# Attention with q left unnormalised: its reciprocal root as a per-row scale of the scores

## The chip, the cores and the metric

The kernel runs on one core of one Trainium2 chip. The metric is the device time of one execution in microseconds. Engines are named as in the profile: PE (TensorE matmul), PEld (its weight loads), DVE (VectorE), ACT (ScalarE), POOL (GpSimd) and SP (SyncE, which issues the transfers here).

## What is computed

The reference is a model of four layers on 1040 tokens (16 meta tokens and 1024 others), width 1024: attention, a matrix LSTM, a gated linear recurrence, attention again. The change touches the two attention layers. In them, cut to what matters:

```python
def rmsnorm(x, g):
    y = x * lax.rsqrt(jnp.mean(x * x, axis=-1, keepdims=True) + EPS)
    return y * g

q, k, v, z = split(u @ w_in)              # 16 q heads, 4 k/v heads of 64
q = rope(rmsnorm(q, q_gain), pos)
k = rope(rmsnorm(k, k_gain), pos)
s = einsum(q, kk) * 64 ** -0.5            # window of 128, blocks of 128 queries
s = where(mask, s, -inf)
m = maximum(s.max(-1), sink)
e = exp(s - m)
p = e / (e.sum(-1) + exp(sink - m))
o = einsum(p, vv)
out = (o * silu(z)) @ w_out
```

The normalisation is per head and per token: over the 64 values of one head.

## The kernel before

Activations lie with features on partitions and tokens along the row. Tokens are cut into three chunks of 400, 384 and 256 columns (`CHUNKS`; the last layer computes q from column 16 on, so its chunks are 384, 384 and 256), and into nine blocks: 16 meta tokens and eight of 128 (`CHUNK_BLOCKS` has four, three and two of them in the three chunks). Every large product is made of three fp32r products of a high and a low part, `proj` at L227: 24 instructions for a tile of 128 features and one chunk.

A q tile (there are eight per attention layer) holds two heads of 64 features. Its way through `qk_proj`, per chunk:

- `evac`: ACT copies the product times the gain column into `dst` (L491) and squares it into `sq` (L492); SP then issues four copies of 32 partitions each into `rot` (L495), the other half of each head for the rope. `dst`, `sq` and `rot` are three of the six buffers of the pool "t" (`tmp`, `TMPS`), which other stages use too.
- `stat`: one f32 product (L506) of a block matrix of ones, 128 x 128, with the squares sums each head's 64 squares and spreads the sum over the head's 64 partitions; ACT makes the reciprocal root in two activations over the whole chunk (L337 Ln, L338 Exp). The first `stat` of a chunk also loads the rope factors `cs` (L503), which have one buffer.
- `rope`: four passes of DVE: times cosine (L511), rotated times sine (L512), sum (L513), times the reciprocal root (L514).
- `q_split`: the high part (ACT, L462) and the low part (DVE, L463), for the two heads, into "qs" buffers (four per chunk size).

K tiles, two per layer, take the same way with their own split (L443 to L446).

The mixers then take, per pair of q tiles, block and head, an `S_step`: four products of q with k (L597, L598) into one PSUM tile, a copy of the sinks by POOL (L602), then for each of the two heads one pass of DVE (L604) that adds the mask, multiplies by -1.0 and takes the minimum with the negated sink, giving the negated scores and minus the maximum; ACT makes the exponential and its sum (L607), DVE the reciprocal (L609), POOL the product (L610). `T_step` transposes (L622) and splits the result (L624, L625); `V_step` multiplies with v (L641).

The order of PE's work is written out as a list of steps, each with a cost in ns (`MM` is 1/2.4 ns a column). Finishing steps are events: `D_Q` gives, in booked ns of PE work behind the end of a tile's projection, when `stat`, `rope` and the split stand. `spread`, `chain` and `weave` put events and fills between the steps; the loop at L723 moves a split behind the last `S_step` that still uses its buffers. Only PE runs in exactly this order (L115); the queues of the other engines are ordered at build time, by the order of the steps, with the mixers' steps raised (`hi`, `PRIO`), and by when their inputs and buffers are ready in the builder's model.

Of the kernel before, what the change touches and what calls it, by code (L numbers as in the profile page):

```python
# [9 lines left out]
F32 = mybir.dt.float32  # L10
F32R = mybir.dt.float32r
AF = mybir.ActivationFunctionType
ALU = mybir.AluOpType
PSUM = bass.MemoryType.PSUM

P = 128
# [7 lines left out]
BIG = -1.0e30  # L24
CHUNKS = [(0, 400), (400, 384), (784, 256)]
LAST_CHUNKS = [(16, 384), (400, 384), (784, 256)]
CHUNK_BLOCKS = [(0, 1, 2, 3), (4, 5, 6), (7, 8)]


def blk(b):  # L30
    return (0, NMETA) if b == 0 else (NMETA + P * (b - 1), P)
# [14 lines left out]
D_V, V_AHEAD, K_AHEAD = 1500.0, 3000.0, 12000.0  # L46
PARTS = 4
FIRST = (0.2, 0.8, 0.85), (0.2, 0.75, 0.8)
D_Q = 2000.0, 4000.0, 6000.0


MM = 1.0 / 2.4
# [58 lines left out]
def hybrid_kernel(ctx: ExitStack, tc: tile.TileContext, ins, out, layers=(0, 1, 2, 3)):  # L111
    nc = tc.nc
    v, s, g, pe, sp = nc.vector, nc.scalar, nc.gpsimd, nc.tensor, nc.sync
# [11 lines left out]
    def nm(x):  # L125
        ctr[0] += 1
        return f"{x}{ctr[0]}"
# [22 lines left out]
    def psa():  # L150
        return psum("pa", 1)
# [7 lines left out]
    eps = cpool.tile([P, 1], F32, name="eps")  # L159
# [19 lines left out]
    def new_mix():  # L179
        if layer_pool[0] is not None:  # L180
            layer_pool[0].close()
        layer_pool[0] = ExitStack()
        return layer_pool[0].enter_context(tc.tile_pool(name=nm("mix"), bufs=1))
# [231 lines left out]
    def layer_a(i, j, first, last, fin):  # L415
        win, wout = ins["a_win"][j], ins["a_wout"][j]
        chunks = LAST_CHUNKS if last else CHUNKS
        R = {}

        def enter():  # L420
            R["mix"] = mix = new_mix()
            R["masks"] = masks = mix.tile([P, 384], F32, name=nm("masks"))
            sp.dma_start(masks, ins["a_masks"])
            R["cons"] = cons = mix.tile([P, 18], F32, name=nm("cons"))
            sp.dma_start(cons, ins["a_cols"][j])
            v.tensor_scalar(cons[:, 0:1], cons[:, 0:1], 0.125, None, op0=ALU.mult)
            v.tensor_scalar(cons[:, 2:18], cons[:, 2:18], -1.0, None, op0=ALU.mult)

        order = {}
# [22 lines left out]
        def q_split(t):  # L452


            def step(qf, n, c0, cn):
                def fn():
                    q = qf()
                    R["q", t, n] = []
                    for hh in range(2):
                        st = R["mix"].tile([P, CHUNKS[n][1]], F32R, tag=f"qs{n}", name=nm("qs"), bufs=4)  # L460
                        hs, os = slice(64 * hh, 64 * hh + 64), slice(64 - 64 * hh, 128 - 64 * hh)
                        s.copy(st[hs, :cn], q[hs])  # L462
                        v.tensor_tensor(st[os, :cn], q[hs], st[hs, :cn].bitcast(F32), op=ALU.subtract)  # L463
                        R["q", t, n].append(st)

                order["q", t, n] = z = [0.0, fn, None]
                return z

            return step
# [12 lines left out]

            return work

        def qk_proj(src, gcol, work, fsplit, ch):
            late = {}

            def evac(acc, n, c0, cn):
                dst, sq, rot = work(n, c0, cn)
                late[n] = dst, sq, rot  # L490
                s.activation(dst, acc[:, :cn], AF.Identity, scale=R["cons"][:, gcol : gcol + 1])  # L491
                s.activation(sq, acc[:, :cn], AF.Square)  # L492
                for q in range(4):
                    o = q ^ 1
                    sp.dma_start(rot[32 * q : 32 * q + 32], dst[32 * o : 32 * o + 32])  # L495

            def finish(n, c0, cn):
                def stat():
                    dst, sq, rot = late[n]
                    b0, bn = CHUNKS[n]  # L500
                    if R.get("cs", (None,))[0] != n:
                        R["cs"] = n, R["mix"].tile([P, 2, 400], F32, tag="cs", name=nm("cs"), bufs=1)
                        sp.dma_start(R["cs"][1][:, :, :bn], ins["rope"][:, :, b0 : b0 + bn].rearrange("a p t -> p a t"))  # L503
                    late[n] = dst, sq, rot, R["cs"][1][:, :, c0 - b0 : c0 - b0 + cn]
                    st = psa()
                    pe.matmul(st[:, :cn], R["masks"][:, 0:P], sq, start=True, stop=True)  # L506
                    rstd_from(st, sq, cn, 64)

                def rope():
                    dst, sq, rot, cos_sin = late[n]  # L510
                    v.tensor_tensor(dst, dst, cos_sin[:, 0, :cn], op=ALU.mult)  # L511
                    v.tensor_tensor(rot, rot, cos_sin[:, 1, :cn], op=ALU.mult)  # L512
                    v.tensor_tensor(dst, dst, rot, op=ALU.add)  # L513
                    v.tensor_tensor(dst, dst, sq, op=ALU.mult)  # L514

                return [(D_Q[0], [4 * cn * MM, stat, None]), (D_Q[1], [0.0, rope, None]),
                        (D_Q[2], fsplit(lambda: late[n][0], n, c0, cn))]

            return proj(src, evac, ch), [finish(n, *c) for n, c in enumerate(ch)]

# [51 lines left out]
        def mixers():  # L572


            def S_step(w):
                mix, cons = R["mix"], R["cons"]
                b, hh, n = w["b"], w["hh"], w["n"]
                kh, kl = R["k", w["pair"] // 2][hh]
                q0, nq = blk(b)
                qb = slice(q0 - chunks[n][0], q0 - chunks[n][0] + nq)  # L580
                if b == 0:
                    k0, kbs = 0, ((0, 0, 16),)
                elif b == 1:
                    k0, kbs = 0, ((0, 0, 16), (1, 16, 128))
                else:
                    k0, kbs = q0 - P, ((b - 1, 0, 128), (b, 128, 128))
                w["kbs"] = kbs
                nk = sum(z[2] for z in kbs)
                kw, mo = (nk if b == 0 else 256), {0: 128, 1: 112}.get(b, 0)
                kb = slice(k0, k0 + kw)  # L590
                S = psum("pm", 2).rearrange("p (u k) -> p u k", u=2)
                w["Sm"] = Sm = mix.tile([P, 2, 257], F32, tag="Sm", name=nm("Sm"), bufs=2)
                st, den = small(2), small(2)
                sinks = []
                for u, t in enumerate(w["ts"]):
                    q = R["q", t, n][hh]
                    pe.matmul(S[:nq, u, :kw], q[:, qb], kh[:, kb], start=True, stop=False)  # L597
                    pe.matmul(S[:nq, u, :kw], q[:, qb], kl[:, kb], start=False, stop=True)  # L598
                    head = (2 * (t // 4) + hh) * 4 + t % 4
                    sinks.append(cons[:nq, 2 + head : 3 + head])  # L600
                    if u == 0:
                        g.tensor_copy(Sm[:nq, :, nk : nk + 1], cons[:nq, 2 + head : 4 + head].rearrange("p (u c) -> p u c", c=1))  # L602
                for u in range(2):
                    v.tensor_tensor_reduce(Sm[:nq, u, :nk], S[:nq, u, :nk], R["masks"][:nq, P + mo : P + mo + nk],  # L604
                                           -1.0, sinks[u], ALU.add, ALU.min, st[:nq, u : u + 1])
                for u in range(2):
                    s.activation(Sm[:nq, u, : nk + 1], Sm[:nq, u, : nk + 1], AF.Exp, scale=-1.0,  # L607
                                 bias=st[:nq, u : u + 1], accum_out=den[:nq, u : u + 1])
                v.reciprocal(den[:nq], den[:nq])  # L609
                g.tensor_tensor(Sm[:nq, :, :nk], Sm[:nq, :, :nk],  # L610
                                den[:nq].rearrange("p (u c) -> p u c", c=1).to_broadcast([nq, 2, nk]), op=ALU.mult)
# [41 lines left out]
            for pair in range(4):  # L653
                for b in range(1 if last else 0, NB):
                    n = [b in z for z in CHUNK_BLOCKS].index(True)
# [3 lines left out]
            for k in range(len(units) + V_LAG):  # L659
                seg = units[k]["pair"] if k < len(units) else 4  # L660
                for lag, cost, fn in ((V_LAG, 480, V_step), (T_LAG, 432, T_step), (0, 480, S_step)):
                    if 0 <= k - lag < len(units):
                        w = units[k - lag]
# [10 lines left out]
        kg1, kfin1 = qk_proj(win[1], 1, tmps, k_split(1), CHUNKS)  # L674
        vg0, vfin0 = v_proj(win[2], 0)
        vg1, vfin1 = v_proj(win[3], 1)
        qg = {t: qk_proj(win[4 + t], 0, tmps, q_split(t), chunks) for t in range(8)}

        def q_pair(p):

# [42 lines left out]
        for i in range(3, 12):  # L723
            for t in (2 * (i // 3), 2 * (i // 3) + 1):
                at = [id(z) for z in body]
                q, k = (at.index(id(z)) if id(z) in at else -1
                        for z in (order["q", t, i % 3], order["S", i // 3 - 1, i % 3]))
# [623 lines left out]
    ahead, k = 0.0, 0  # L1351
# [6 lines left out]
    k = 0  # L1358
# [31 lines left out]
def _layout(inp):  # L1390
    f = {}
# [3 lines left out]
    am = np.zeros((P, 384), np.float32)  # L1395
    am[:64, :64] = 1.0
    am[64:, 64:128] = 1.0
    ii = np.arange(P)[:, None]
    jj = np.arange(256)[None]
    am[:, 128:] = np.where((jj > ii) & (jj <= ii + P), 0.0, BIG)  # L1400
    f["a_masks"] = am
    f["b_mask"] = np.where(ii <= np.arange(P)[None], 0.0, BIG).astype(np.float32)
    f["ident"] = np.eye(P, dtype=np.float32)
# [7 lines left out]
    for j in range(2):  # L1411
        w = np.asarray(inp["a_w_in"])[j]
# [7 lines left out]
        qg, kg = np.asarray(inp["a_q_gain"])[j], np.asarray(inp["a_k_gain"])[j]  # L1420
# [7 lines left out]
    q0, k0, v0, i0, f0, o0, z0 = np.cumsum([0, 1024, 1024, 2048, 8, 8, 2048])  # L1428
# [27 lines left out]
    masks = np.zeros((P, 6, 32), np.float32)  # L1456
# [22 lines left out]
```

## Time and profile before

| | |
|---|---|
| three runs, us | 2633.74, 2634.56, 2635.0 |
| median | 2634.56 us |
| profiled execution, span from first to last instruction | 2630.8 us, 53986 instructions |
| mean granted clock of PE | 0.995 |
| layer 0 (attention) | about 0 to 445 us of the span |
| layer 3 (attention) | about 2200 us to the end |

For the profiled execution the profile gives the span; no other time of it is known. The span lies 3.8 us under the median of the runs.

How to read it: times are in us from the span's start, unless marked ns. A group line reads: line of the kernel, engine, operation, output <- inputs by the program's names, shape, count | busy us in all, mean ns of one | idle time of the engine just before them and what ended most of it. A line of the waits reads: who waited <- for whom: us in all, times, longest. In order of time: start, duration, engine, line, operation, and in brackets the engine's idle time before it and what ended it. Matmuls are pipelined: one lasts longer than the distance to the next.

### The profile page before, as it was taken

The page shows a single profiled execution, that of the slowest core. Times are in us where ns is not written, and L with a number is a line of the kernel's source. Part 1 is how long each engine was busy: PE and PEld are TensorE (multiplying, and loading weights), DVE is VectorE, ACT ScalarE, POOL GpSimd, SP SyncE. Part 2 cuts the span into 40 slices and gives each one's busy share as a digit, 9 for nine tenths or more (in the row PEclk, how much of TensorE's full clock was granted, in tenths as well). Part 3 has the DMA queues.
Part 4 walks back from the last instruction along what each step waited for, and adds up shares of the span by engine and source line. Part 5 has one row for each costly group of instructions (what it writes and reads, how often), then busy time and mean ns, then how long its engine had stood idle before and what let it go on. Part 6 is the DMA issues. An engine that isn't in the chain of part 4 may idle for free.

```text
span 2630.8 us, 53986 instructions
## 1 busy us (share of the span) xinstructions
PE 2562.9 (97%) x20246; PEld 2468.6 (94%) x20246; DVE 1976.8 (75%) x5344; ACT 1693.7 (64%) x4374; POOL 249.5 (9%) x502
## 2 busy tenths in 40 slices
PE   7999999989999999999999999999999999999999
PEld 5899989989999999999999999999999998999999
DVE  7887798784747474757475688988888989887896
ACT  7777767565454545454545757878675857867772
POOL 2221231000000000000000000101000000321330
PEclk9999999999999999999999999999999999999999
DMA  4213111011111111111111101111110113212112
GB/s 129 69 49 91 47 44 48 22 63 52 41 57 41 57 41 57 41 53 45 53 45 49 53 30 42 34 34 34 38 38 30 38 50 92 63 39 83 55 37 80
DMA packets 82581, 135.89 MB, mean 52 GB/s; under 512 B 12032, under 2 KB 35712, under 8 KB 82320
## 3 DMA queue, kind: packets, MB, share of 16 engines
q1 hardware_dynamic: 82320, 132.45, 15.9%
q8 instruction: 159, 2.61, 0.4%
q14 instruction: 102, 0.84, 0.1%
HBM read 117.56 MB, written 4.26 MB: 46 GB/s over the span
## 4 chain that ended last, share of the span: by engine, by line
PE 74%; DVE 12%; ACT 8%; DMA 3%; issue 2%; SPq 1%; POOL 1%; DVEq 0%; ACTq 0%; POOLq 0%
PE pj L227 35%; PE pj L321 15%; PE pj L276 10%; ACT Sm L607 1%; PE po L641 1%; PE po L885 1%; PE pt L622 1%; PE pa L899 1%; PE po L887 1%; DVE Sm L604 1%; DVE wl L194 1%; DMA cs<-in_rope 1%; PE pj L272 1%; DVE Pl L625 1%; PE pm L1137 1%
## 5 line engine op out<-in xcount | busy, mean ns | idle before, releaser
L227 PE MATMUL pj<-uh,wh 128*128 128x256 f32 (+2 forms) x2688 | 919.7, 342 | 9.4 <-ACT uh L193 9.4
L227 PE MATMUL pj<-ul,wh 128*128 128x256 f32 (+2 forms) x2688 | 867.2, 323 | 2.7 <-DVE ul L194 2.4
L227 PE MATMUL pj<-uh,wl 128*128 128x256 f32 (+2 forms) x2688 | 863.8, 321 | 0.0
L227 PEld LDWEIGHTS pj<-uh,wh 128*128 128x128 f32 x2688 | 509.3, 189 | 28.6 <-ACT uh L193 13.1
L227 PEld LDWEIGHTS pj<-ul,wh 128*128 128x128 f32 x2688 | 509.5, 190 | 13.8 <-DVE ul L194 6.4
L227 PEld LDWEIGHTS pj<-uh,wl 128*128 128x128 f32 x2688 | 509.0, 189 | 0.1
L193 ACT CAST wh<-wr 128x512 fp32r<-128x512 f32 (+1 forms) x338 | 202.9, 613 | 102.0 <-PE pj L321 31.3
L194 DVE TENSOR_TENSOR wl<-wr,wh 128x512 fp32r<-128x512 f32 (+1 forms) x338 | 232.1, 697 | 48.5 <-ACT wh L193 45.0
L321 PE MATMUL pj<-yh,wh 128*128 128x384 f32 (+2 forms) x768 | 253.1, 330 | 9.9 <-DVE x L324 6.4
L324 DVE TENSOR_TENSOR x<-x,pj 128x384 f32<-128x384 f32 (+2 forms) x480 | 234.6, 509 | 34.1 <-PE pj L321 32.7
L321 PE MATMUL pj<-yl,wh 128*128 128x384 f32 (+2 forms) x768 | 245.3, 319 | 0.3 <-DVE yl L194 0.3
L321 PE MATMUL pj<-yh,wl 128*128 128x384 f32 (+2 forms) x768 | 245.2, 319 | 0.0
L276 PE MATMUL pj<-wh,uh 128*128 128x256 f32 (+1 forms) x768 | 231.9, 302 | 0.0
L276 PE MATMUL pj<-wl,uh 128*128 128x256 f32 (+1 forms) x768 | 216.5, 282 | 0.0
L276 PE MATMUL pj<-wh,ul 128*128 128x256 f32 (+1 forms) x768 | 216.2, 281 | 0.0
L607 ACT ACTIVATE Sm<-Sm,s 128x257 f32<-128x257 f32 (+2 forms) x272 | 130.7, 482 | 91.7 <-DVE s L604 90.3
L610 POOL TENSOR_TENSOR Sm<-Sm,s 128x512 f32<-128x512 f32 (+2 forms) x136 | 141.2, 1038 | 467.1 <-DVE s L609 454.3
L403 ACT ACTIVATE t<-t 128x384 f32<-128x384 f32 (+2 forms) x240 | 117.8, 491 | 88.0 <-DVE t L402 86.4
L402 DVE SCALAR_TENSOR_TENSOR t<-pj,t 128x384 f32<-128x384 f32 (+2 forms) x192 | 98.8, 515 | 81.7 <-ACT t L401 80.0
L321 PEld LDWEIGHTS pj<-yh,wh 128*128 128x128 f32 x768 | 144.2, 188 | 14.7 <-DVE x L324 8.6
L193 ACT CAST yh<-r 128x384 fp32r<-128x384 f32 (+2 forms) x120 | 57.1, 478 | 146.2 <-PE pj L321 132.5
L276 PEld LDWEIGHTS pj<-wh,uh 128*128 128x128 f32 x768 | 144.6, 188 | 2.1
(251 smaller groups left out, 5445.7 us busy)
## 6 DMA issues: line engine op xcount, KB each, us to landing
wr<-in_b_win SPq DMA_DIRECT2D x124, 256.0 KB, 2.8
wr<-in_a_win SPq DMA_DIRECT2D x80, 256.0 KB, 2.9
wr<-in_c_win SPq DMA_DIRECT2D x64, 256.0 KB, 2.8
wr<-in_a_wout SPq DMA_DIRECT2D x32, 256.0 KB, 2.8
wr<-in_b_wout SPq DMA_DIRECT2D x32, 256.0 KB, 2.7
t<-t SPq DMA_DIRECT2D x104, 48.0 KB, 2.0
cs<-in_rope SPq DMA_DIRECT2D x11, 400.0 KB, 3.7
cs<-in_rope SPq DMA_DIRECT2D x11, 384.0 KB, 3.2
```

Of the source, the lines that this page charges most:

```text
L193: s.copy(h, src)
L194: v.tensor_tensor(l, src, h.bitcast(F32), op=ALU.subtract)
L227: pe.matmul(acc[:, :cn], a[:, k, :], b[:, k, c0 : c0 + cn], start=(k == 0 and i == 0), stop=(k == KT - 1 and i == 2))
L272: pe.matmul(acc[:48, :nc], um[0][:, k, :], m[:, kk, :], start=(k == 0 and m is wh), stop=(k == KT - 1 and m is wl))
L276: pe.matmul(acc[:cn, :nc], a[:, k, c0 : c0 + cn], m[:, kk, :], start=(k == 0 and j == 0), stop=(k == KT - 1 and j == 2))
L321: pe.matmul(acc[:, :cn], a[:, k, mc], b, start=(k == 0 and i == 0), stop=(k == 1 and i == 2))
L324: v.tensor_tensor(x[:, m, c0 : c0 + cn], x[:, m, c0 : c0 + cn], acc[:, :cn], op=ALU.add)
L402: v.scalar_tensor_tensor(a[:, :cn], z, 0.0, a[:, :cn], op0=ALU.min, op1=ALU.subtract)
L403: s.activation(a[:, :cn], a[:, :cn], AF.Exp)
L604: v.tensor_tensor_reduce(Sm[:nq, u, :nk], S[:nq, u, :nk], R["masks"][:nq, P + mo : P + mo + nk], -1.0, sinks[u], ALU.add, ALU.min, st[:nq, ...
L607: s.activation(Sm[:nq, u, : nk + 1], Sm[:nq, u, : nk + 1], AF.Exp, scale=-1.0, bias=st[:nq, u : u + 1], accum_out=den[:nq, u : u + 1])
L610: g.tensor_tensor(Sm[:nq, :, :nk], Sm[:nq, :, :nk], den[:nq].rearrange("p (u c) -> p u c", c=1).to_broadcast([nq, 2, nk]), op=ALU.mult)
```

## The change

Per q tile and chunk the reciprocal root is no longer multiplied into q. `rope` and the split work on the unnormalised q, and the score pass multiplies each query's row by that query's reciprocal root. For that the sums of squares have to lie with queries on partitions: `stat_q` takes, for each block of 128 tokens, the squares of that block as the stationary operand and two columns of the block matrix (one per head) as the moving one, so that one column per head and block comes out; the two activations run on these columns, two per block, into `rq`. The sign that the score pass gave by -1.0 moves into the gain column (-0.125), and the mask's constant is positive. The loading of the rope factors becomes a step of its own, `factors`, and q has four event times of its own; K keeps the three old ones.

```diff
-D_Q = 2000.0, 4000.0, 6000.0
+D_K = 2000.0, 4000.0, 6000.0
+D_Q = 1500.0, 2500.0, 3500.0, 4500.0
...
-            v.tensor_scalar(cons[:, 0:1], cons[:, 0:1], 0.125, None, op0=ALU.mult)
+            v.tensor_scalar(cons[:, 0:1], cons[:, 0:1], -0.125, None, op0=ALU.mult)
...
+                def stat_q():
+
+                    sq = late[n][1]
+                    nb = len(CHUNK_BLOCKS[n])
+                    R["rq", t, n] = rq = R["mix"].tile([P, 2 * nb], F32, tag=f"rq{n}", name=nm("rq"), bufs=4)
+                    st = psa()
+                    for k, b in enumerate(CHUNK_BLOCKS[n]):
+                        if last and b == 0:
+                            continue
+                        q0 = blk(b)[0] - c0
+                        pe.matmul(st[:, 2 * k : 2 * k + 2], sq[:, q0 : q0 + P], R["masks"][:, 0:P:64], start=True, stop=True)
+                    z = slice(2 if last and n == 0 else 0, 2 * nb)
+                    s.activation(rq[:, z], st[:, z], AF.Ln, bias=eps, scale=1.0 / 64)
+                    s.activation(rq[:, z], rq[:, z], AF.Exp, scale=-0.5)
...
-                    v.tensor_tensor(dst, dst, sq, op=ALU.mult)
-
-                return [(D_Q[0], [4 * cn * MM, stat, None]), (D_Q[1], [0.0, rope, None]),
-                        (D_Q[2], fsplit(lambda: late[n][0], n, c0, cn))]
+                    if t is None:
+                        v.tensor_tensor(dst, dst, sq, op=ALU.mult)
+
+                turn = fsplit(lambda: late[n][0], n, c0, cn)
+                if t is not None:
+                    return [(D_Q[0], [0.0, factors, None]), (D_Q[1], [108 * len(CHUNK_BLOCKS[n]), stat_q, None]),
+                            (D_Q[2], [0.0, rope, None]), (D_Q[3], turn)]
+                return [(D_K[0], [4 * cn * MM, stat, None]), (D_K[1], [0.0, rope, None]), (D_K[2], turn)]
...
                 for u in range(2):
+                    rq = R["rq", w["ts"][u], n][:nq, 2 * kq + hh : 2 * kq + hh + 1]
                     v.tensor_tensor_reduce(Sm[:nq, u, :nk], S[:nq, u, :nk], R["masks"][:nq, P + mo : P + mo + nk],
-                                           -1.0, sinks[u], ALU.add, ALU.min, st[:nq, u : u + 1])
+                                           rq, sinks[u], ALU.add, ALU.min, st[:nq, u : u + 1])
...
-    am[:, 128:] = np.where((jj > ii) & (jj <= ii + P), 0.0, BIG)
+    am[:, 128:] = np.where((jj > ii) & (jj <= ii + P), 0.0, -BIG)
```

More of the change, by code (lines that the diff above doesn't have):

```diff
@@ L483, in work_rows, with qk_proj @@
             return work
-        def qk_proj(src, gcol, work, fsplit, ch):
+        def qk_proj(src, gcol, work, fsplit, ch, t=None):
             late = {}
@@ L497, in finish, with factors @@
             def finish(n, c0, cn):
-                def stat():
-                    dst, sq, rot = late[n]
+                def factors():
                     b0, bn = CHUNKS[n]
@@ L503, in stat @@
                         sp.dma_start(R["cs"][1][:, :, :bn], ins["rope"][:, :, b0 : b0 + bn].rearrange("a p t -> p a t"))
-                    late[n] = dst, sq, rot, R["cs"][1][:, :, c0 - b0 : c0 - b0 + cn]
+                    late[n] += (R["cs"][1][:, :, c0 - b0 : c0 - b0 + cn],)
+                def stat_q():
[11 more added lines that the diff above has]
+                    s.activation(rq[:, z], rq[:, z], AF.Exp, scale=-0.5)
+                def stat():
+                    factors()
+                    sq = late[n][1]
                     st = psa()
@@ L580, in S_step @@
                 qb = slice(q0 - chunks[n][0], q0 - chunks[n][0] + nq)
+                kq = CHUNK_BLOCKS[n].index(b)
                 if b == 0:
@@ L676, in layer_a @@
         vg1, vfin1 = v_proj(win[3], 1)
-        qg = {t: qk_proj(win[4 + t], 0, tmps, q_split(t), chunks) for t in range(8)}
+        qg = {t: qk_proj(win[4 + t], 0, tmps, q_split(t), chunks, t) for t in range(8)}
         def q_pair(p):
```

## The prediction

> **What bounds the kernel now.** I read the page first, for its span and busy shares.
>
> ```profile
> span 2630.8 us, 53986 instructions
> PE 2562.9 (97%) x20246; PEld 2468.6 (94%) x20246; DVE 1976.8 (75%) x5344; ACT 1693.7 (64%) x4374; POOL 249.5 (9%) x502
> ```
>
> TensorE is the bound, busy 97%. Only the two attention layers are edited, so the second view is the busy time by stage: the start of layer 0, its body, and layer 3's body. Columns: window, length, then busy us of PE, PEld, DVE, ACT, POOL, granted clock, DMA share, GB/s.
>
> ```profile
> 0.00:70.00 70.00, 51.59 (x197) 39.57 (x198) 50.23 (x96) 50.55 (x106) 14.55 (x21) 0.93 0.39 124
> 70.00:445.00 375.00, 362.22 (x2458) 346.48 (x2458) 308.87 (x859) 282.35 (x783) 91.75 (x144) 1.00 0.20 59
> ...
> 2200.00:2570.00 370.00, 355.07 (x2380) 340.20 (x2380) 311.51 (x809) 277.26 (x734) 87.01 (x127) 1.00 0.22 64
> ```
>
> In the attention bodies PE is idle 375 - 362.2 = 12.8 us and 370 - 355.1 = 14.9 us; VectorE is busy 82% and 84%, ScalarE 75%. In the first 70 us PE is idle 18.4 us. So relief of VectorE and ScalarE can give back at most 28 us in the bodies and some of the 18 at the start; every us added to PE's stream counts almost in full. Third, I asked who stops PE in each body (who waits for whom: total us, times, longest), and for one such stop in order of time.
>
> ```profile
> PE pt L622 <- POOL Sm L610: 4.3, 4, 2.1
> PE pa L506 <- ACT t L492: 3.8, 3, 1.8
> ...
> 256.08 0.70 PE L506 MATMUL pa<-t,masks 128*128 128x256 f32 x2 [1.82 <-ACT t L492]
> ...
> PE pa L506 <- ACT t L492: 5.5, 4, 2.2
> PE pj L321 <- DVE x L324: 2.4, 3, 1.4
> ```
>
> The first two lines and the stop are layer 0, the last two layer 3. The largest single stop, 3.8 + 5.5 = 9.3 us in 7 waits, is the very product that is replaced (L506), waiting for its squares (L492). One of the seven, the 1.82 us at 256.08, belongs to the second K tile, which runs there; the q tiles own 7.5 us.
>
> **The change part by part.** There are 8 q tiles x 3 chunks x 2 layers = 48 finishes.
>
> *PE, removed.* One f32 product shows as two instructions.
>
> ```profile
> L506 PE MATMUL pa<-t,masks 128*128 128x384 f32 x52 | 22.1, 507 | 2.5 <-ACT t L492 2.5
> L506 PE MATMUL pa<-t,masks 128*128 128x256 f32 x36 | 12.0, 417 | 6.9 <-ACT t L492 6.7
> L506 PE MATMUL pa<-t,masks 128*128 128x400 f32 x20 | 8.4, 503 | 0.0
> L506 PE MATMUL pa<-r,masks 128*128 128x400 f32 x4 | 1.7, 497 | 0.0
> L506 PE MATMUL pa<-r,masks 128*128 128x256 f32 x4 | 1.2, 377 | 0.0
> ```
>
> 52 + 36 + 20 = 108 instructions are 54 products: 48 of q and 6 of the second K tile, so q has 8 of 400 columns, 24 of 384, 16 of 256. The two undisturbed rows give the stream price: (497 - 377) / 144 = 0.833 ns a column and instruction, 1.667 ns a column for the pair. Removed: 8 x 0.667 + 24 x 0.640 + 16 x 0.427 = 27.5 us.
>
> *PE, added.* Now the squares are the stationary operand, one block of 128 columns at a time, against two columns. 9 blocks x 8 tiles in layer 0 and 8 x 8 in layer 3 are 136 products, 272 instructions, each with its own weight load and almost no stream. No row shows this shape; the load must set the pace.
>
> ```profile
> L597 PEld LDWEIGHTS pm<-r,qs 128*16 128x16 f32 x16 | 1.4, 94 | 2.4 <-DVE x L324 2.4
> ...
> L506 PEld LDWEIGHTS pa<-r,masks 128*128 128x128 f32 x12 | 2.1, 188 | 0.0
> L804 PEld LDWEIGHTS pt<-ident,r 8*128 8x128 f32 x8 | 1.0, 136 | 0.0
> ...
> 540.84 0.20 PE L804 MATMUL pt<-ident,r 8*128 8x8 f32 x1
> 540.90 0.20 PE L805 MATMUL pt<-ident,r 8*128 8x8 f32 x1
> ...
> 271.23 0.17 PE L598 MATMUL pm<-r,qs 128*16 128x16 f32 x1
> ...
> 263.46 0.28 PE L227 MATMUL pj<-uh,wh 128*128 128x256 f32 x1
> ...
> 264.50 0.28 PE L227 MATMUL pj<-uh,wh 128*128 128x256 f32 x1
> ```
>
> A load of 16 columns lasts 94 ns, one of 128 columns 188 ns: 94 / 112 = 0.84 ns a column, 107 ns for 128. The transposes at L804 and L805 load 128 columns in 136 ns and follow each other every 0.06 us, so a load does run under its neighbours; but they are the quicker transposing load. The nine steps of L227 from 263.46 to 264.50 take 0.116 us each, with the 188 ns load and a stream of 107 ns under it. Bounds: 0.06 us gives 272 x 0.06 = 16.3 us (PE -11), 0.116 us gives 31.6 us (PE +4). A load not hidden at all, 0.188 + 0.17 us (the product of 16 columns at L598 lasts 0.17), would give 97 us (+70); L804 speaks against it. I take 0.116, because the load is L506's kind. **PE: +4 us**. (The step list books 108 ns a product, under half of my 232.)
>
> [...]
>
> *ScalarE.* The logarithm and the exponential shrink from a chunk to 2 columns a block.
>
> ```profile
> L337 ACT ACTIVATE t<-pa,eps 128x384 f32<-128x384 f32 x37 | 21.3, 575 | 1.2 <-PE pa L506 0.9 <-PE pa L1234 0.2
> L338 ACT ACTIVATE t<-t 128x384 f32<-128x384 f32 x37 | 19.4, 524 | 0.5
> L1025 ACT ACTIVATE s<-s,one 128x8 f32<-128x8 f32 x3 | 0.8, 288 | 0.0
> L1024 ACT ACTIVATE s<-s 128x8 f32<-128x8 f32 x3 | 0.5, 204 | 0.0
> ```
>
> 575 + 524 becomes about 288 + 204 (rows of 8 columns, with and without a bias column): 0.6 us less in each of the 32 long finishes, two thirds of that in the 16 of 256 columns: 26 us in all, against 282 + 277 us that ScalarE is busy in the bodies, between 4 and 5%.
>
> *VectorE.* The multiply by the root (L514) goes; the score pass (L604) reads its scale from a column instead of -1.0.
>
> ```profile
> L514 DVE TENSOR_TENSOR t<-t,t 128x384 f32<-128x384 f32 x26 | 15.8, 607 | 0.9 <-ACT t L338 0.3
> L514 DVE TENSOR_TENSOR t<-t,t 128x256 f32<-128x256 f32 x18 | 8.4, 465 | 0.3
> L604 DVE CUSTOM_DVE_ANT_0 Sm<-pm,masks,cons 128x256 f32<-128x256 f32 x224 | 99.9, 479 | 3.6 <-PE pm L598 2.6
> L402 DVE SCALAR_TENSOR_TENSOR t<-pj,t 128x256 f32<-128x256 f32 x64 | 26.8, 420 | 4.9 <-ACT t L401 4.7
> L904 DVE SCALAR_TENSOR_TENSOR C<-C,wb,pa 128x257 f32<-128x257 f32 x56 | 26.9, 480 | 60.2 <-PE pa L899 60.2
> ```
>
> Gone: 32 x 0.607 + 16 x 0.465 = 27 us. A second column operand is not shown. L402 has a constant and L904 a column, on like shapes with one PSUM side: 60 ns apart, so from 0 to 272 x 0.06 = 16 us; below nothing is excluded, as a column cannot spare work. I take 0: L604 already fetches its sink from a column. Even 16 us would leave VectorE lighter.
>
> *Waits and buffers.* The product now stands 2500 ns of booked PE work behind its projection (2000 before), rope at 3500 (4000), the split at 4500 (6000). Each finish holds three of the six "t" buffers: the squares until 4000 and more before, 2500 now; the rotated copy 4000, now 3500; the result 6000, now 4500. That is 14,000 against 10,500 buffer-ns. At the longest wait the two evacuations of one chunk stand 1.9 us apart, with other work of ScalarE between:
>
> ```profile
> 2383.12 0.48 ACT L491 ACTIVATE t<-pj,cons 128x256 f32<-128x256 f32 x1
> ...
> 2385.00 0.36 ACT L492 ACTIVATE t<-pj 128x256 f32<-128x256 f32 x1
> ...
> 2385.42 1.22 PE L506 MATMUL pa<-t,masks 128*128 128x256 f32 x2 [2.16 <-ACT t L492]
> ```
>
> I read this as the squares waiting for a free buffer. With 0.5 us more room, a lighter ScalarE and earlier freed buffers I take 5 of q's 7.5 us away. The other PE waits of the bodies, 27.7 - 9.3 = 18 us, mostly hang on the same two engines; with 4 to 5% less work on each, and queues that shorten faster than work does, I take 3 us. At the start PE waits for ScalarE's casts of the normed rows:
>
> ```profile
> PE pj L227 <- ACT uh L193: 9.1, 7, 3.8
> ```
>
> Four q finishes fall there, each 1.2 us lighter on ScalarE and VectorE together: I take 2 of these 4.8 us. The new wait, L604 for the column of roots, costs nothing: it follows the 2500 point by two short activations, and the scores need the split at 4500 anyway.
>
> The transfer of the rope factors, 11 times per chunk size as before, now stands at 1500 instead of 2000 in SP's queue; the rope that frees its one buffer moves as far, from 4000 to 3500. The distance stays, and weight loads wait behind it as before: 0.
>
> **Sum:** +4 - 5 - 3 - 2 = -6 us against the span 2630.8, so 2624.8. The runs' median, 2634.56, lies 3.8 us above the span; forecast 2628.5.
>
> **Rivals.**
>
> *Cheap loads* (chance 0.12). If the plain load also repeats every 0.06 us, PE gains 11 instead of losing 4: 2628.5 - 15 = 2613.5. For it stands L804; against it 188 ns beside 136.
>
> *Nothing but PE counts* (0.20). PE-bound stretches hand relief to later stops: the four waits of PE on L324 and L610 above are not q's. Then +4 and the stops come back elsewhere: 2638, inside the bound of no change.
>
> *Slower: the rope arrives before its data* (0.25). Behind each evacuation SP issues four copies, then they land:
>
> ```profile
> L495 SPq DMA_DIRECT2D t<-t x216: 507/588/1381, 29.6 to 2489.2; - x108
> ...
> DMA to landing us min/median/max: 1.7/1.9/3.9
> ...
>   DMA t<-t: 2.6, 4
> ```
>
> 0.48 (L491 above) + 4 x 0.59 + 1.9 = 4.7 us, later than either rope point; VectorE's queue is in order, so a rope put 0.5 us earlier holds scores, splits and x updates behind it 0.5 us longer: 48 x 0.5 = 24 us of VectorE, whose idle in both bodies is 66 + 58 us. If two thirds reach PE, +16: 2628.5 + 16 = 2644.5. The last line is VectorE's idle ahead of the rope's first line, L511, until such a copy lands: 2.6 us in 4 stops now. The rival decides once that is above some 15 us. Against it: VectorE's queue is ordered at build time by readiness, so the rope may simply stay where it was.
>
> *Unhidden loads* (0.02): +70 in place of +4, 2628.5 + 66 = 2694.5. [...]
>
> **How the numbers follow.** A measurement of this kernel tells about 0.2%, 5.3 us, from no change: faster is below 2629.3, slower above 2639.8. The forecast has 0.41; its terms may each miss by 2 to 4 us, some 6 together, so a little over half of it lies below 2629.3 and the rest in the band. Faster: 0.12 + 0.23 = 0.35. No change: 0.18 of the forecast, 0.13 of "only PE" and 0.04 of the slower case = 0.35. Slower: 0.07 + 0.21 + 0.02 = 0.30. The range takes in cheap loads and the slower rival, 2612 to 2646; the likeliest case's own is 2622 to 2635.
>
> **What would show it.** Right: the new product's instructions 0.116 us apart; L506's waits under 4 us, K's share left; ScalarE and VectorE each some 25 us less busy; L604 near 479 ns. Wrong: 0.06 us or over 0.2 us spacing; L604 near 540; more VectorE idle ahead of the rope; PE stops grown at L622, L321 or L597 by what L506 lost.

## The result, and the profile after

The changed kernel takes 2630.86 us in the median (2624.5 to 2634.16, 7 runs) against 2634.56 before: ratio 0.9984, 95% interval 0.9973 to 0.9995. That is 3.7 us, inside the 0.2% that the prediction counts as no change, though the interval lies below 1. Its runs spread over 10 us, those of before over 2.5. The profiled execution is the slowest of the seven (2634.16 us), so its span lies above the one of before (2630.8) although the median lies below.

The page of the changed kernel (span; busy time, share and instructions of each engine):

```profile
span 2632.4 us, 54257 instructions
PE 2570.6 (98%) x20422; PEld 2488.0 (95%) x20422; DVE 1976.7 (75%) x5296; ACT 1667.5 (63%) x4374; POOL 249.6 (9%) x502
```

ScalarE is 26 us less busy, as forecast. VectorE's busy time is the same: 1976.8 before, 1976.7 now. The stages, with the columns of the prediction's table:

```profile
0.00:70.00 70.00, 51.36 (x214) 41.16 (x215) 48.33 (x92) 48.13 (x105) 14.30 (x21) 0.91 0.39 124
70.00:445.00 375.00, 366.74 (x2529) 355.10 (x2529) 308.90 (x838) 270.69 (x782) 94.03 (x144) 0.99 0.20 59
...
2200.00:2570.00 370.00, 358.75 (x2464) 349.58 (x2463) 314.25 (x792) 268.83 (x740) 85.10 (x127) 0.99 0.21 65
```

PE's idle time in the two bodies falls from 27.7 to 8.3 + 11.3 = 19.5 us, by 8.2. Who stops PE (total us, times, longest); the first four lines are layer 0, the rest layer 3:

```profile
PE pt L647 <- POOL Sm L635: 2.8, 4, 1.5
PE pm L621 <- DVE Pl L650: 2.0, 1, 2.0
PE po L666 <- DVE v L587: 1.4, 1, 1.4
PE pa L525 <- ACT t L493: 0.9, 1, 0.9
...
PE pt L647 <- POOL Sm L635: 2.9, 2, 2.6
PE pj L322 <- DVE x L325: 2.6, 2, 2.1
...
PE pa L516 <- ACT t L493: 0.2, 1, 0.2
```

The stops for the squares are gone: 9.3 us before, now 0.9 (K's, L525) and 0.2 (q's new product, L516). That is the whole 8.2. All other stops of the bodies were 27.7 - 9.3 = 18.4 us and are 19.5 - 1.1 = 18.4 us. Now the prices, as groups and, for the pace of the product, in order of time:

```profile
L516 PE MATMUL pa<-masks,t 128*128 128x2 f32 x272 | 34.4, 242 | 0.2 <-ACT t L493 0.2
L516 PEld LDWEIGHTS pa<-masks,t 128*128 128x128 f32 x272 | 36.4, 197 | 0.6 <-ACT t L493 0.6
...
147.78 0.59 PE L516 MATMUL pa<-masks,t 128*128 128x2 f32 x4
148.23 0.43 PE L228 MATMUL pj<-uh,wh 128*128 128x400 f32 x1
...
L629 DVE CUSTOM_DVE_ANT_0 Sm<-pm,masks,cons 128x256 f32<-128x256 f32 x224 | 114.2, 539 | 2.8 <-PE pm L622 1.7 <-PE pj L228 0.3
```

Four instructions of the product take 148.23 - 147.78 = 0.45 us, 0.1125 us each. The score pass, L604 before and L629 now, went from 479 to 539 ns. Times 272, that is 16 of the 27 us that VectorE lost with the multiply. The other 11 do not show in its busy time either: passes that the change does not touch last longer, the rope's cosine product on the t rows 33.1 us in all instead of 29.7 and the low part of the split 56.5 instead of 54.0 (L511 and L463 before, L530 and L464 now). Why they do, and what makes up the rest, is not shown.

One thing was not in the sum: the granted clock. Windows of 2 us (the column before the last two is the clock), first before, then after:

```profile
2384.00:2386.00 2.00, 0.58 (x1) 0.50 (x2) 2.00 (x7) 2.00 (x7) 0.12 (x1) 0.82 0.52 168
2386.00:2388.00 2.00, 2.00 (x7) 1.89 (x6) 1.90 (x4) 1.95 (x6) 1.01 (x1) 0.50 0.35 131
2388.00:2390.00 2.00, 2.00 (x11) 1.99 (x10) 1.91 (x4) 1.89 (x5) 0.00 (x0) 0.83 0.19 48
```

```profile
358.00:360.00 2.00, 0.06 (x1) 0.00 (x0) 1.94 (x5) 0.22 (x1) 0.85 (x2) 1.00 0.00 0
360.00:362.00 2.00, 1.96 (x13) 1.96 (x14) 1.96 (x8) 0.96 (x5) 0.00 (x0) 0.73 0.00 0
362.00:364.00 2.00, 2.00 (x9) 1.51 (x8) 0.98 (x2) 0.29 (x3) 0.32 (x2) 0.50 0.00 0
364.00:366.00 2.00, 2.00 (x14) 2.00 (x14) 1.21 (x5) 0.30 (x2) 0.09 (x1) 0.92 0.00 0
```

In both a stop of PE of about 2 us (2.16 for the squares, 1.98 for VectorE's L650) is followed by some 3.4 us at about half clock, which costs PE another 1.7 us while it counts as busy. Adding 2 us x (1 - clock) over the windows below 0.9 from 60 to 448 and from 2190 to 2582 gives 5.1 us before and 13.1 after. The stop of before at 2384 is gone; others have come, at the start (88 to 91), here at 360, and in layer 3 (2208 to 2214 and 2504 to 2508).

### The profile page after: what moved, and what is told of

It is laid out like the page before. It is cut to its first block, busy times and chain, and to the rows that moved or that the text cites. A ratio compares the mean times of both kernels' runs of the same rounds, so it can differ in the third digit from the quotient of the medians.

```text
span 2632.4 us, 54257 instructions
## 1 busy us (share of the span) xinstructions
PE 2570.6 (98%) x20422; PEld 2488.0 (95%) x20422; DVE 1976.7 (75%) x5296; ACT 1667.5 (63%) x4374; POOL 249.6 (9%) x502
## 4 chain that ended last, share of the span: by engine, by line
PE 76%; DVE 12%; ACT 7%; issue 2%; DMA 2%; POOL 1%; SPq 0%; DVEq 0%; ACTq 0%; POOLq 0%
PE pj L228 36%; PE pj L322 16%; PE pj L277 10%; PE po L666 2%; PE pt L647 1%; ACT Sm L632 1%; PE po L910 1%; PE pa L924 1%; DVE wl L195 1%; PE po L912 1%; DVE Sm L629 1%; PE pj L273 1%; DVE qs L464 1%; DVE Pl L650 1%; PE pm L1162 1%
## 5 line engine op out<-in xcount | busy, mean ns | idle before, releaser
L325 DVE TENSOR_TENSOR x<-x,pj 128x384 f32<-128x384 f32 (+2 forms) x480 | 234.9, 508 | 34.5 <-PE pj L322 33.0
L322 PEld LDWEIGHTS pj<-yh,wh 128*128 128x128 f32 x768 | 145.1, 189 | 13.6 <-DVE x L325 8.5
```

The source lines that it names most:

```text
L322: pe.matmul(acc[:, :cn], a[:, k, mc], b, start=(k == 0 and i == 0), stop=(k == 1 and i == 2))
L325: v.tensor_tensor(x[:, m, c0 : c0 + cn], x[:, m, c0 : c0 + cn], acc[:, :cn], op=ALU.add)
```

## The experiments

My theory: the change wins the stops for the squares, because the root's chain on ScalarE and VectorE is shorter, and gives half or more back through the column, 60 ns on VectorE in each score pass, and through stops that halve the clock. Rivals: the moved times made the gain ("later time"); fewer buffers held (the prediction's reading); TensorE's instructions alone count.

| kernel | median us | kernel before, run beside it, us | difference, us | ratio, 95% interval |
|---|---|---|---|---|
| changed, once more (after_again) | 2630.67 | 2635.39 | -4.7 | 0.9981, 0.9973 to 0.999 |
| e1 times alone | 2643.37 | 2635.39 | +8.0 | 1.003, 1.0018 to 1.0041 |
| e2 changed, old times | 2630.24 | 2635.39 | -5.2 | 0.998, 0.9971 to 0.9989 |
| e3 changed, constant scale | 2622.25 | 2635.39 | -13.1 | 0.9946, 0.9934 to 0.9959 |
| e4 changed, products twice | 2649.25 | 2635.27 | +14.0 | 1.0051, 1.0035 to 1.0066 |
| e5 changed, rounded squares | 2624.96 | 2635.27 | -10.3 | 0.996, 0.9947 to 0.9972 |
| e6 before, rounded squares | 2636.62 | 2635.27 | +1.4 | 1.0006, 0.9997 to 1.0015 |
| e8 before, column | 2637.61 | 2635.27 | +2.3 | 1.0009, 1.0001 to 1.0018 |
| e9 changed, ScalarE back | 2629.5 | 2635.22 | -5.7 | 0.9977, 0.9969 to 0.9986 |
| e10 changed, buffer held | 2633.94 | 2635.22 | -1.3 | 0.9996, 0.9987 to 1.0004 |
| e11 changed, VectorE back | 2638.09 | 2635.22 | +2.9 | 1.001, 1.0001 to 1.0019 |
| e12 before, no root | 2624.93 | 2635.22 | -10.3 | 0.9959, 0.9947 to 0.9972 |

Where I say "against the changed kernel", I take the difference in this table less -4.7. In e3 and e12 the scores lack the root, so these two time a kernel that computes something else.

**The changed kernel once more.**

> The changed kernel once more, unchanged, on the chip that the other kernels of this group run on, so that they can be held against it. Expected 2624 to 2635 us, 0 to 10 us below the kernel before, as its seven runs lay. If the stops of TensorE at the starts of the attention layers make the spread, the granted clock of a run goes with its time: about 2 us for each stop of 2 us or more that is followed by half the clock.

It came out as expected, -4.7 us. Its profiled execution has a span of 2626.6 us, the first one's was 2632.4, and the two let me see what the spread is made of: following equal products through both traces, the second gains 1.4 us near 2210 and 1.5 us near 2505, where the first had half clock and the second has less or none (by the sum above 9.9 us against 13.1), 0.8 near 1625, 0.9 near 1655, 0.5 near 2125 and the rest in smaller steps. So about half of this difference is the clock. That the spread of all runs is the same thing is likely, not shown.

Followed the same way against the kernel before, the second trace shows where the gain stands. It is 0.6 us behind from 600 to 1500, again 0.5 behind at 2380, 3.4 ahead right after it, and 4.2 ahead at 2580. The step of 3.9 us is the stop before 2385.42 with its half clock, 2.16 + 1.7 us. In this pair of traces the net gain is that one stop; what the other stops gave is paid back elsewhere.

**The times alone, and the change at the old times.**

```
e1 (before):  +D_Q = 2500.0, 3500.0, 4500.0   # product, rope, split of q; factors at 1500
              K: D_K = 2000.0, 4000.0, 6000.0
e2 (changed): -D_Q = 1500.0, 2500.0, 3500.0, 4500.0
              +D_Q = 2000.0, 2000.0, 4000.0, 6000.0
```

> The kernel before with q's events moved to the change's times alone (factors 1500, product of the squares 2500, rope 3500, split 4500); the root is still spread over 128 rows and multiplied into q, with K's events as before. Theory 'later time': the product waited for squares that ScalarE had not yet written, and the 500 later due time alone takes q's waits before the product from 7.5 us to under 2 us over the layers, so that this kernel is 3 to 5 us faster than the kernel before. Rival 'fewer buffers held' (the prediction's own step): the squares came late since a buffer was late, the buffers held are hardly fewer here, and the waits stay at 6 us or more; the time stays within 2 us of before. Rival 'rope before its data': the split is 1500 earlier and VectorE waits more ahead of the rope; 2 to 10 us slower.

> The changed kernel with q's events back at the old times (factors and two-column products at 2000, rope 4000, split 6000); the arithmetic is the change's. Theory 'later time': the waits before the two-column products come back to 5 us or more over the layers, and the kernel is 3 to 5 us slower than the changed one, so at or up to 2 us above the kernel before. Rival 'fewer buffers held': the waits stay under 2 us and the time stays within 2 us of the changed kernel. If the stops at the layers' starts come from the earlier split, they are not here: the first V product of layer 0 ends near 89 us, as before, and not at 94.

The waits of PE for the squares in e1 (layer 0, layer 3) and in e2 (layer 0, then two of layer 3):

```profile
PE pa L511 <- ACT t L493: 4.0, 4, 2.3
...
PE pa L511 <- ACT t L493: 6.0, 7, 1.6
```

```profile
PE pa L525 <- ACT t L493: 0.3, 1, 0.3
...
PE pa L516 <- ACT t L493: 1.7, 2, 1.4
...
PE pa L525 <- ACT t L493: 0.4, 1, 0.4
```

"Later time" falls on both: 500 later, the old product waits 10.0 us (9.3 before); at the old time the new one waits 1.7. The gain is in the arithmetic. The times alone cost 8.0 us. That lies in the rope rival's range, but its mechanism is too small: VectorE's idle time ahead of the rope's first line, until a rotated copy lands, goes from 2.6 us before to 6.1 in e1, where the prediction put the bound at some 15. By the sum of the clock e1 loses 10.1 us against 5.1; what else makes the 8.0 is not shown. With the change's arithmetic the times are worth nothing (e2 and the changed kernel 0.5 us apart). The first V product of layer 0 ends at 92.6 us in e2, between 89.3 before and 94.6 in the changed kernel, so the earlier split explains only part of the late start.

**The column taken out, and the column put into the kernel before.**

```
e3 (changed): v.tensor_tensor_reduce(Sm..., S..., masks...,
              -    rq, sinks[u], ALU.add, ALU.min, ...)
              +    1.0, sinks[u], ALU.add, ALU.min, ...)
e8 (before):  -    -1.0, sinks[u], ...
              +    R["neg"][:nq], sinks[u], ...      # a column of -1.0
```

> The changed kernel with the constant 1.0 in place of the column of roots in the score pass, so the root is left out of the scores; its products, logarithms and exponentials still run. Theory 'the column costs': the pass of 128x256 goes from 539 back to 479 ns, VectorE's busy time falls by 272 x 60 ns = 16 us, and as the scores' chain (product, pass, exponential) ends late in places the kernel is 2 to 5 us faster than the changed one. Rival 'VectorE is covered': 16 us off VectorE, and the time within 1.5 us of the changed kernel, as VectorE is busy only three quarters of the span.

> The kernel before with the constant -1.0 of the score pass replaced by a column that holds -1.0: the same result by the same instructions, one operand fetched from a column. If the column alone makes the 60 ns, the pass of 128x256 goes from 479 to 539 ns and VectorE's busy time up by 16 us; by the theory 'the column costs time' the kernel is 5 to 10 us slower than the kernel before, as the column's removal from the changed kernel was worth 8 us. Rival 'only the wait for the root's column, or the root in place of a constant, costs': 479 ns and no more than 1.5 us.

The pass in e3, and in e8:

```profile
L628 DVE CUSTOM_DVE_ANT_0 Sm<-pm,masks,cons 128x256 f32<-128x256 f32 x224 | 100.8, 479 | 3.2 <-PE pm L622 2.1
```

```profile
L606 DVE CUSTOM_DVE_ANT_0 Sm<-pm,masks,cons 128x256 f32<-128x256 f32 x224 | 113.7, 539 | 3.3 <-PE pm L600 2.3
```

The column alone makes the 60 ns. Its price in time depends on the kernel around it: 8.4 us out of the changed kernel, more than the 2 to 5 that I expected, and 2.3 us into the kernel before, less than the 5 to 10 expected. There PE waits 10.4 us for the squares all the same (4.5 + 5.9). e3 also frees the score pass from waiting for the roots, but in the changed kernel VectorE never stands idle ahead of that pass for them. How VectorE's time reaches PE is seen at the stop near 358, in e3's windows and waits:

```profile
358.00:360.00 2.00, 0.93 (x9) 0.83 (x9) 1.97 (x9) 0.29 (x2) 0.14 (x1) 1.00 0.00 0
360.00:362.00 2.00, 2.00 (x15) 1.71 (x14) 1.94 (x6) 1.18 (x7) 0.38 (x2) 1.00 0.00 0
```

```profile
PE pm L621 <- DVE x L325: 1.1, 1, 1.1
```

The stop is 1.1 us, not 2.0, and the clock stays at 1.00. Between the profiled executions of the changed kernel (2626.6) and e3 (2622.4) the lead of 4.2 us arises here: in the median over 40 us it is 0.2 us from 320, 3.6 from 360 and 4.1 from 400 on. The medians lie 8.4 apart; where the other half falls, this pair of traces can't show.

**TensorE's side: the products twice, and with rounded squares.**

```
e4 (changed): +for _ in range(2):
                  pe.matmul(st[:, 2*k : 2*k+2], sq[:, q0 : q0+P], masks[:, 0:P:64], ...)
e5 (changed): s.activation(sq.bitcast(F32R), acc[:, :cn], AF.Square)
              pe.matmul(st[...], sq[...].bitcast(F32R), R["mr"], ...)   # two columns of ones, F32R
e6 (before):  the same squares; pe.matmul(st[:, :cn], R["mr"], sq.bitcast(F32R), ...)
```

> The changed kernel with each two-column product of the squares issued twice into the same place: 272 more TensorE instructions and nothing else. Theory 'TensorE is the bound where these stand, at 0.1125 us each': 272 x 0.1125 = 31 us above the changed kernel, near 2661 us. Rival 'the products fill idle time': under 15 us above it. Rival 'they cost their full duration of 0.242 us': 66 us above it.

> The changed kernel with q's squares and the two columns of ones rounded to the reduced type (fp32r), so that each two-column product is one TensorE instruction and not two: 136 fewer instructions; the squares are less exact. At 0.1125 us each that is 15 us below the changed kernel, near 2615 us. If an instruction of the reduced type costs as much as the two of full type (its weight load the same 0.11 us twice), the time stays within 3 us of the changed kernel.

> The kernel before with q's squares and its 128x128 ones rounded to the reduced type, one TensorE instruction of one pass per chunk in place of two of two passes; the logarithm is taken in PSUM in place and the root is rounded, the spread over 128 rows and the multiply into q stay. TensorE loses some 20 of q's 27.5 us. Theory 'the chain of squares, root and multiply makes the waits': the waits before the product stay at 5 us or more and 15 to 20 us are won, near 2617 us. Rival 'TensorE's gain turns into waits for ScalarE and VectorE, which are as busy as before': less than 10 us are won.

e4 adds 18.7 us against the changed kernel for 272 instructions that keep PE busy 28.7 us more (2594.2 against 2565.5 in after_again), between the first two expectations: some of it fills stops, and no product of the squares waits there any more. In e5 one product is one instruction at the same pace:

```profile
142.76 0.36 PE L518 MATMUL pa<-mr,t 128*128 128x2 f32 x2
142.99 0.43 PE L228 MATMUL pj<-uh,wh 128*128 128x400 f32 x1
```

That is 0.115 us each, so 136 fewer are 15.6 us, and PE's busy time is 13.6 us less (2551.9); the time falls by 5.6, to 2625.0, the quickest here that computes all of it, though with less exact squares. I had expected 15. q's products wait 3.1 us there (0.5 in after_again). In e6 the product of 384 columns is one instruction, and the next product starts 0.18 us behind it (58.19 to 58.37), where the prediction's rows give 0.64 us for the f32 pair; that the difference is one of passes, no view shows. PE is busy 15.0 us less there than in the kernel before (2547.9 against 2562.9) and nothing is won. The waits in layer 0, and in layer 3:

```profile
PE pa L511 <- ACT t L494: 7.5, 3, 4.9
...
PE pa L511 <- ACT t L494: 7.8, 5, 3.1
```

q's products now wait 15.3 us for the squares, where q had 7.5, K's 4.7, where it had 1.8, and by the sum of the clock 13.4 us are lost against 5.1. The rival with "less than 10" was right and my 15 to 20 wrong: with the old chain what PE saves comes back as waits and half clock.

**What of the chain: each part put back, and all of it left out.**

```
e9  (changed): after the two activations on rq, the same two into a spare tile
e10 (changed): rope(): + v.tensor_copy(small(1), sq[:, 0:1])
e11 (changed): rope(): + v.tensor_tensor(rot, dst, dst, op=ALU.mult)
e12 (before):  q: - rstd_from(st, sq, cn, 64)   - v.tensor_tensor(dst, dst, sq, op=ALU.mult)
```

> The changed kernel with the logarithm and exponential of each chunk's roots computed a second time into a spare tile that nobody reads: 48 x (0.265 + 0.207) = 22.7 us more on ScalarE, nearly the 26 us that the change took off it. Theory 'ScalarE's time on the squares' chain made the waits': the waits before the two-column products come back to 4 us or more and the kernel is 5 to 12 us slower than the changed one. Rival 'buffers', or 'ScalarE is covered': within 2 us of the changed kernel, waits under 2 us.

> The changed kernel with one element per row of the squares read again on VectorE at the end of the rope, so that their buffer is held until there as it was before; 48 small copies, some 3 to 5 us of VectorE. Theory 'fewer buffers held' (the prediction's step): the waits before the products come back to 4 us or more, and the kernel is 3 to 6 us slower than the changed one. Rival 'the buffers do not bind': waits under 2 us, within 2.5 us of the changed kernel, the small copies' own price.

> The changed kernel with a multiply of q's size put back at the end of the rope, its product written over the rotated copy, which nobody reads any more: the 27 us of VectorE that the change took away come back, behind the rope and ahead of nothing but the queue. If VectorE's time counts at half its length, as the column's 16 us did by the run without it (8 us), the kernel is 13 us slower than the changed one. Rival 'VectorE has room': less than 4 us slower.

> The kernel before with the logarithm, the exponential and the multiply by the root left out for q, so its scores lack the root; the 128-row product of the squares on TensorE is still issued, and nobody reads it. ScalarE loses some 51 us and VectorE 27, TensorE nothing. Theory 'the chain on ScalarE and VectorE sets the bodies' time': 13 to 20 us faster than the kernel before, with TensorE's instructions unchanged, and the waits before the product under 2 us. Rival 'TensorE is the bound': no more than the 7.5 us of q's waits.

e9: within 1.0 us of the changed kernel, q's product waits 1.0 us. The added activations last 22.5 us, but ScalarE's busy time rose only 11.5 us (1678.4 against 1666.9), since neighbours overlap (in the changed kernel the exponential at 58.62 lasts 0.21 us and the next activation starts at 58.73); so it tests less than I meant. e10: 3.4 us above the changed kernel, at the edge, since the two intervals overlap. What is longer is not q's wait but K's, 2.8 us against 1.2 in after_again (layer 0, layer 3, then q's):

```profile
PE pa L525 <- ACT t L493: 2.1, 1, 2.1
...
PE pa L525 <- ACT t L493: 0.7, 1, 0.7
...
PE pa L516 <- ACT t L493: 0.3, 1, 0.3
```

So the held buffer of the squares is not what kept q's squares late, and in e2 the two other buffers are due to be held as long as before. e11: 24.0 us more of VectorE (1999.9 against 1975.9) cost 7.6 us, near a third, between the two expectations; q's wait is 0.7 us. e12, with TensorE's instructions as before:

```profile
PE pa L506 <- ACT t L492: 0.4, 1, 0.4
...
PE pa L506 <- ACT t L492: 2.2, 2, 1.2
```

2.6 us of waits are left of 9.3, and 10.3 us are won, more than q's waits, less than the 13 that I expected. The chain makes the waits. Which part of it does is open: neither 11.5 us of ScalarE, nor 24 of VectorE, nor the buffer of the squares alone brings them back. More buffers were not tried.

## Why the prediction was nearly right, and where it was wrong

The forecast, 2628.5, missed by 2.4 us, but not every term held.

- **PE +4: right as a price.** 0.1125 us an instruction, 0.116 forecast. Loads of 197 ns over the whole array follow each other every 0.1125 us, and the prediction's steps of L227, a load of the whole array and 256 columns each, every 0.116. Wrong was "every us added to PE's stream counts almost in full": two thirds counted in e4 (18.7 of 28.7), 41% came back in e5 (5.6 of 13.6), nothing in e6.
- **The stops for the squares, -5: right, and somewhat low** (q's from 7.5 to 0.2, in after_again 0.5). Of the reasons given, more room is excluded (e1, e2), and so are earlier freed buffers as the sole cause (e10 for the squares', e2 for the others); the lighter chain stands (e12).
- **The other stops, -3: did not come.** They are 18.4 us before and after; ScalarE's relief did not shorten them, and VectorE's did not exist. In e3, where VectorE is 16 us lighter, PE's whole idle time in the bodies is 14.8 us, with no wait for the squares: about the 3 us.
- **The column, 0: the step that failed.** The bounds were right and the upper one, 16 us, is what it measures; the row that gave it (L402 beside L904) had the 60 ns. The reason for the lower end, "L604 already fetches its sink from a column", was no reason, as the second column costs by itself (e8). And "even 16 us would leave VectorE lighter" was wrong: busy time is the same to 0.1 us, in part as other passes last longer. In time the column takes 8.4 us, and VectorE's 24 us in e11 are worth 7.6, so the multiply's removal and the column about cancel.
- **The start, -2: wrong.** Near 90 us the changed kernel is 5.3 us late; the clock takes part of it (half clock until 74 instead of 71, and again from 88 to 91). Of that lag 1.4 us is left at 430 in after_again.
- **The total, in part by luck.** The stops gave 7 us and not 5, the terms of 3 and 2 us did not come, and the column's time and the half clock were not in the sum; these errors go both ways. The 3.8 us from span to median are doubtful too: in both profiled executions of the changed kernel the time lies 1.8 us above the span, so the one of before was likely some 2 us quicker than its median.
- **The rivals.** "Cheap loads" and "unhidden loads" fall by the pace. "Nothing but PE counts" falls by e12, which wins 10.3 us with PE's instructions unchanged. "The rope arrives before its data" falls in the changed kernel by its own measure: VectorE's idle time ahead of the rope until a rotated copy lands is 4.7 and 4.2 us in the two traces, 2.6 before, where it needed some 15.

The range held the time, and so did the band of no change, which had a chance of 0.35.

## What to carry to other kernels

An engine busy 97% is not the bound wherever it waits: 15.0 us off TensorE's busy time gave nothing on the old chain, and 13.6 us gave 5.6 on the new one, so take an engine's busy time off and see what the stage gives before counting it in full. When an operand goes from a constant to a column, price it by the two rows that differ in just that, and multiply by the count; if the engine was to be relieved, set that against the relief. Moving a chain's due times was worth nothing here with the short chain and cost 8 us with the long one: shorten first, then move.

## What the runs showed of the hardware

A second column in place of a constant costs the score pass some 60 ns at each of its widths: 479 to 539 ns for 256 columns, 363 to 421 for 144, 217 to 279 for 16 (the kernel before and the changed kernel; e8, where nothing but the column is new, has 539 for 256 columns).

Half clock followed some stops of about 2 us here and not others, and where it followed one of those at 358, 2384 and 2502 us it lasted 3.41 us. The length of the stop does not decide it alone: the 1.98 us at 358 were followed by half clock and e3's 1.1 us there were not, but neither were the 2.12 us before 127.06 in the kernel before, nor the 2.62 us before 2239.01 in the changed kernel. The two traces of the changed kernel part near 2500: in the first PE waits 2.13 us for L325 before 2503.36, and the clock falls to 0.62 in the window behind; in the second PE is idle 1.15 us of the window from 2498, and the clock stays at 1.00. Their windows, first and second trace:

```profile
2502.00:2504.00 2.00, 0.64 (x4) 0.65 (x5) 1.97 (x5) 0.00 (x0) 0.35 (x2) 1.00 0.00 0
2504.00:2506.00 2.00, 2.00 (x10) 2.00 (x10) 1.55 (x4) 0.00 (x0) 0.00 (x0) 0.62 0.00 0
...
2498.00:2500.00 2.00, 0.85 (x5) 0.85 (x6) 1.97 (x5) 0.00 (x0) 0.14 (x1) 1.00 0.00 0
2500.00:2502.00 2.00, 2.00 (x16) 2.00 (x15) 1.99 (x8) 0.01 (x1) 0.00 (x0) 1.00 0.00 0
```

In the traces of the kernel before and of the changed kernel the recorded clock changes only on a grid of 3.413 us: in the changed kernel half clock begins at 87.86, 360.93, 2207.54 and 2504.50 us, which are 80, 541 and 87 steps apart. The five stops of these two traces named here differ in how much of them falls inside one step. The 2.13 us before 2503.36 lie whole in the step from 2501.09 to 2504.50, the 1.98 us before 360.04 whole in the one from 357.51 to 360.93, and 2.02 of the 2.16 us before 2385.42 in the one that ends at 2385.28; half clock begins at the end of each of these steps. The 2.12 us before 127.06 are parted at 125.65 into 0.71 and 1.40, the 2.62 us before 2239.01 at 2238.26 into 1.87 and 0.75, and no half clock follows. So a stop of 2 us cost nearly twice its time here or not, in keeping with where it lay, and the 1.5 us near 2505 are a part of the difference between the two traces of the changed kernel. Why the clock falls, and from which length on, is not shown: 1.81 us of idle time in the step from 1651.17 of the changed kernel were followed by half clock, the 1.87 us above were not.
